# Strassen's seven products for the input projection of layer 0 in a two-layer float32 decoder trunk

## The chip, the core and the metric

The kernel runs on one core of one Trainium2 chip. What is compared is device time in microseconds (us) from launch to end. The core has five engines that run in parallel and wait for each other by semaphores: PE (TensorE, matrix products), DVE (VectorE), ACT (ScalarE), POOL (GpSimd) and SP, whose queue issues the transfers between DRAM and the on-chip memory (SBUF). Products land in PSUM, eight banks of 128 x 512 float32 values, and DVE or ACT read them from there.

## What is computed

The input x has 1024 tokens of 1024 features. Two layers and a last norm follow; only layer 0 changes. Of the reference, cut to what matters:

```python
def even_mixer(y, w_in, w_pool, pool_scale, conv_w, w_out):
    proj = y @ w_in                                   # 1024 x 1024 times 1024 x 6144
    u_a, gate_b, gate_c, h_c, z = jnp.split(proj, [...], axis=-1)
    pooled = causal_multiscale_pool(...)              # four groups, windows 2, 4, 8, 16
    a = jnp.einsum("bsgc,gcd->bsgd", pooled, w_pool).reshape(b, s, POOL_WIDTH) * pool_scale
    cu = gate_c * h_c
    v = conv_w[2] * cu + conv_w[1] * shift_right(cu, 1) + conv_w[0] * shift_right(cu, 2)
    bo = gate_b * v
    out = jnp.concatenate([a, bo], axis=-1) * jax.nn.silu(z)
    return out @ w_out

h = h + even_mixer(rms_norm(h, norm_g[0]), ...)       # layer 0
h = h + odd_mixer(rms_norm(h, norm_g[1]), ...)        # layer 1: sliding-window attention
return rms_norm(h, final_norm_g)
```

Every matrix product is made of float32 values that are split into a high part, rounded to fp32r, and the low rest; ah·bh + ah·bl + al·bh stands for a·b. So one product of a 128 x 128 block of weights with 512 tokens is three matmuls (`mm3`, L178 to L184).

## The kernel before

The projection's 6144 output features are 48 column tiles of 128. A tile of weights is 128 x 8 x 128 (eight blocks of 128 input features); it comes in by one transfer of 512 KB, ACT casts its high part and DVE subtracts for the low part (`split`, L174 to L176). `take` (L285 and on) keeps loads some three tiles and splits one tile ahead of the products.

- Operands of layer 0: x comes in transposed (`xT`, features on the partitions) in 16 loads of 128 x 512 (`load_x`, L354). ACT multiplies by the norm's gain and rounds (`uH`, L359), DVE makes the low part (`uL`, L360). The norm's factor 1/rms of each token is not applied there but later, to the outputs (`r_b`, `r2_b`), since it is one factor a token; the squares for it (L366 to L369) run beside the first products.
- Start: eight matmuls on zeros (`WARM`, L398), then two column tiles on the first 512 tokens, block by block as the loads arrive (L411 to L413), then a third and a fourth tile.
- Then the 48 tiles in an order written out by hand: for each of four pooling groups two tiles of `u` and two gates, for each of eight convolution tiles j the tiles 16+j, 24+j, 40+j, 8+j. `proj` (L386) makes a tile as two halves of 512 tokens, each 8 blocks x 3 matmuls = 24. After a tile DVE multiplies by `r_b` and does the pooling or convolution, ACT the silu, POOL some multiplications. The small products of the pooling groups (`mix`, L482) are 24 matmuls a group. The gated outputs `o` stay in SBUF.
- Output projection: `operands` (L540) splits `o`, then L564 to L566 make 8 tiles x 2 halves, 48 matmuls each.

The order on PE is the program's. DVE, ACT and SP follow the program's order at the start (`order()`, until the loads of x are through); after that a scheduler sets their order when the kernel is built. The rest, layer 1, is not changed.

Of the kernel before, what the change touches and what calls it, by code (L numbers as in the profile page):

```python
# [32 lines left out]
WARM = 8       # matmuls before the first loads arrive, for the clock of the tensor engine  # L33
SQ = 6         # squares of the first half wait for this tile
# [11 lines left out]
# columns of the per-channel parameter array  # L46
# [29 lines left out]
def trunk(ctx, tc, xT, pos, cols, w_in, w_pool, w_out, w_q, w_kv, w_z, b_q, b_kv,  # L76
# [8 lines left out]
    big = ctx.enter_context(tc.tile_pool(name="big", bufs=16))  # L85
    ps = ctx.enter_context(tc.tile_pool(name="ps", bufs=4, space=PSUM))

    # h1 + b_out: per half, 32 features of 512 tokens each
    h1_dram = tc.dram_tile([2, D // 32, HALF, 32], F32, name="h1_dram")

    turn = [0]

    def psA(name=None):
        turn[0] += 1
        return ps.tile([P, HALF], F32, name=name or ("psA", "psD")[turn[0] % 2], bufs=2)

    def psB(dtype=F32):
        return ps.tile([P, HALF], dtype, name="psB")

# [47 lines left out]
    def diag_r(rcol, s):  # L147
        """the 512 values of half s, high and low, on the diagonals of four blocks"""
# [29 lines left out]
    def mm3(dst, parts):  # L178
        """dst = sum over (ah, al, bh, bl) of ah'bh + ah'bl + al'bh."""
# [70 lines left out]
    # ================= layer 0 =================  # L250
    wp = tc.alloc_tile_pool(name="wp", bufs=9, side="right")

    # weights in the order of use: raw tiles are loaded three units ahead, split one unit ahead
    def wtile(shape):
        return lambda d: wp.tile(shape, d, name="W")

    units = []      # (source, raw shape, how to allocate a part, parts)
# [7 lines left out]
    def load_to(n):  # L265
        while len(raws) < min(n, len(units)):
            src, shape, _, _ = units[len(raws)]
            raws.append(wp.tile(shape, F32, name="W"))
# [25 lines left out]
    for m in (32, 33):  # L294
        unit(w_in[m], KP)
    for g in range(1, 4):
        unit(w_in[2 * g], KP)
        unit(w_pool[g - 1], [P, 2, 256])
        for m in (2 * g + 1, 32 + 2 * g, 33 + 2 * g):
            unit(w_in[m], KP)  # L300
    for j in range(8):
        unit(w_in[16 + j], KP)
        if j == 0:
            unit(w_pool[3], [P, 2, 256])
        for m in (24 + j, 40 + j, 8 + j):
            unit(w_in[m], KP)
# [7 lines left out]
    def u_tile(shape):  # L314
        return lambda d: big.tile(shape, d, name="U")
# [4 lines left out]
    for s in range(2):  # L320
        for m in range(KT):
            if s == 0 and m == 0:
                unit(w_z[m], KP, u_tile(KP))
            elif s == 1 and m >= ZLATE:
                unit(w_z[m], KP, lambda d: big.tile([P, 4, P], d, name="O0"), parts=2)
# [8 lines left out]

    order()
    with tc.tile_pool(name="l0", bufs=4) as p0:
        def T():
            return p0.tile([P, 16 + S], F32, name="T", bufs=4)

        def t2(dtype=F32):  # L340
            return p0.tile([P, HALF], dtype, name="t2", bufs=5)

        def big2(s, dtype=F32):
            return big.tile([P, HALF], dtype, name=f"O{s}")

        r_b = p0.tile([P, S], F32, name="r_b", bufs=1)
        r2_b = p0.tile([P, S], F32, name="r2_b", bufs=1)

        uH = [big.tile([P, S], F32R, name="U") for _ in range(KT)]
        uL = [big.tile([P, S], F32R, name="U") for _ in range(KT)]  # L350

        heads, loads = [], []

        def load_x(s, k):  # L354
            xin = big2(s)
            loads.append(nc.sync.dma_start(out=xin, in_=xT[k * P:(k + 1) * P, hs(s)]))
            if s == 0 and k == 0:
                nc.sync.dma_start(out=colt, in_=cols)
            heads.append(act(out=uH[k][:, hs(s)], in_=xin, func=AF.Copy, scale=col(C_G1, k)))  # L359
            stt(out=uL[k][:, hs(s)], in0=xin, scalar=col(C_G1, k),  # L360
                in1=uH[k][:, hs(s)].bitcast(F32), op0=ALU.mult, op1=ALU.subtract)
            return xin

        def squares(xs, add):
            acc = t2()
            act(out=acc, in_=xs[0], func=AF.Square)  # L366
            for x in xs[1:]:
                act(out=x, in_=x, func=AF.Square)
                add(out=acc, in0=acc, in1=x, op=ALU.add)  # L369
            return acc  # L370

        def stats0(s, acc):
            rsqrt_mean(const, rcol0[:, 4 * s:4 * s + 4], col_sums(acc), 4)

        def spread0(s):
            bank = spread_r(diag_r(rcol0, s), psB() if s == 0 else psA())
            nc.scalar.copy(out=r_b[:, hs(s)], in_=bank)
            tt(out=r2_b[:, hs(s)], in0=bank, in1=r_b[:, hs(s)], op=ALU.mult)
# [6 lines left out]
        pre = {}  # L385

        def proj(m):
            if m in pre:
                return pre.pop(m)
            w = take()  # L390
            return [proj_half(w, s) for s in range(2)]

        # keep the tensor engine busy, for its clock, while the first loads arrive
        bank, idle = psB(), t2()[:, 0:HALF // 2]
        nc.vector.memset(idle, 0.0)
        idle = idle.bitcast(BF16)
        for _ in range(WARM):
            mm(bank, lhsT=idle[:, 0:P], rhs=idle, start=True, stop=True)  # L398

        # start: three weight tiles on the first half while the second half arrives  # L400
        ws = [[wp.tile(KP, d, name="W") for d in (F32, F32R, F32R)] for _ in range(2)]
# [603 lines left out]
```

## Time and profile before

| | |
|---|---|
| time, median of 3 runs | 1157.64 us (1156.61 to 1157.99) |
| span of the profiled execution | 1158.2 us, 0.56 us above that median |
| PE busy | 1126.6 us, 97% |
| DVE, ACT, POOL busy | 619.2, 386.6, 272.6 us |
| moved by DMA | 83.92 MB, 72 GB/s over the span |

The page gives the profiled execution's span alone, from the first to the last instruction. Busy time is the union of an engine's instructions; a matmul's shown duration includes its way through the array, so on PE the distance from start to start tells the rate. The granted clock of PE is a share of 2.4 GHz: 1.00 is that level, 0.5 is 1.2 GHz.

### The profile page before, as it was taken

How to read it: one execution, taken by the hardware profiler on the slowest of the kernel's cores; microseconds unless marked ns; L12 is line 12 of the kernel's file. 1: busy time of each engine (PE TensorE's matmuls, PEld its weight loads, DVE VectorE, ACT ScalarE, POOL GpSimd, SP SyncE). 2: the span in 40 equal slices, each digit the busy share in tenths (PEclk: the TensorE clock that was granted, in tenths of full speed). 3: DMA queues.
4: the chain of work that ended last, by engine and by line, in shares of the span. 5: the costliest groups of instructions: out<-in, count | busy, mean ns of one | idle time of the engine just before them, and what ended most of it. 6: DMA issues, size and time to landing. Idle time of an engine off the chain costs nothing.

```text
span 1158.2 us, 14036 instructions
## 1 busy us (share of the span) xinstructions
PE 1126.6 (97%) x5248; PEld 921.5 (80%) x5248; DVE 619.2 (53%) x1109; ACT 386.6 (33%) x797; POOL 272.6 (24%) x427
## 2 busy tenths in 40 slices
PE   9999999999999999999999999999999998898897
PEld 6788888888888888888888788898888886677676
DVE  7993637332233223223655865641133669899995
ACT  8132122111111111111432532420012687776653
POOL 1200000010010110110101100143330036787874
PEclk9899999999999999999999999999999999999999
DMA  7111111111111111111144344520022405460001
GB/s 242 45 47 55 46 52 49 55 41 51 55 37 55 55 37 55 54 38 64 59 148 148 110 164 144 177 80 1 19 69 95 146 19 120 64 90 21 19 19 55
DMA packets 59892, 83.92 MB, mean 72 GB/s; under 512 B 36272, under 2 KB 37424, under 8 KB 59824
## 3 DMA queue, kind: packets, MB, share of 16 engines
q1 hardware_dynamic: 59824, 83.03, 23.4%
q8 instruction: 41, 0.67, 0.2%
q14 instruction: 27, 0.22, 0.1%
HBM read 74.63 MB, written 8.39 MB: 72 GB/s over the span
## 4 chain that ended last, share of the span: by engine, by line
PE 85%; DVE 8%; ACT 3%; issue 1%; DMA 1%; SPq 1%; POOL 0%; ACTq 0%; DVEq 0%
PE psB L184 8%; PE psB L183 8%; PE psB L182 8%; PE psA L184 5%; PE psA L183 5%; PE psA L182 5%; PE psD L184 5%; PE psD L183 5%; PE psD L182 5%; PE psA L566 2%; PE psA L564 2%; PE psA L565 2%; PE psD L566 2%; PE psD L564 2%; PE psD L565 2%
## 5 line engine op out<-in xcount | busy, mean ns | idle before, releaser
L175 ACT CAST W<-W 128x1024 fp32r<-128x1024 f32 (+2 forms) x109 | 107.4, 988 | 531.7 <-DVE W L176 427.0
L176 DVE TENSOR_TENSOR W<-W 128x1024 fp32r<-128x1024 f32 (+2 forms) x109 | 125.4, 1155 | 235.6 <-PE psB L183 177.8
L183 PE MATMUL psB<-U,W 128*128 128x512 f32 x384 | 152.6, 397 | 2.0 <-DVE U L360 1.8
L184 PE MATMUL psB<-U,W 128*128 128x512 f32 x384 | 152.7, 398 | 0.0
L182 PE MATMUL psB<-U,W 128*128 128x512 f32 x384 | 150.7, 392 | 0.0
L183 PEld LDWEIGHTS psB<-U,W 128*128 128x128 f32 x384 | 72.9, 190 | 20.8 <-DVE U L360 4.0
L521 POOL TENSOR_TENSOR T<-T,r_b 128x1024 f32<-128x1024 f32 x8 | 19.3, 2416 | 290.6 <-DVE T L519 290.6
L182 PEld LDWEIGHTS psB<-U,W 128*128 128x128 f32 x384 | 72.9, 190 | 16.4
L184 PEld LDWEIGHTS psB<-U,W 128*128 128x128 f32 x384 | 73.1, 190 | 14.5
L184 PE MATMUL psD<-U,W 128*128 128x512 f32 x184 | 72.5, 394 | 0.0
L184 PE MATMUL psA<-U,W 128*128 128x512 f32 x184 | 72.5, 394 | 0.0
L183 PE MATMUL psD<-U,W 128*128 128x512 f32 x184 | 72.2, 392 | 0.0
L183 PE MATMUL psA<-U,W 128*128 128x512 f32 x184 | 72.1, 392 | 0.0
L182 PE MATMUL psA<-U,W 128*128 128x512 f32 x184 | 71.5, 389 | 0.0
L182 PE MATMUL psD<-U,W 128*128 128x512 f32 x184 | 71.4, 388 | 0.0
L582 POOL TENSOR_TENSOR t<-t,T 128x512 f32<-128x512 f32 x14 | 19.2, 1370 | 170.5 <-ACT T L581 170.5
L734 ACT ACTIVATE pt<-psB,smax 128x128 f32<-128x128 f32 x128 | 45.5, 367 | 25.0 <-DVE smax L731 21.6
L722 PE MATMUL psB<-kT,qT 128*128 128x256 f32 (+1 forms) x128 | 35.2, 297 | 17.3 <-ACT qT L703 9.4
L875 PE MATMUL psD<-O,aH 128*128 128x512 f32 (+1 forms) x128 | 51.1, 399 | 0.0
L566 PE MATMUL psA<-U,W 128*128 128x512 f32 x128 | 50.4, 394 | 0.5 <-DVE W L176 0.5
L566 PE MATMUL psD<-U,W 128*128 128x512 f32 x128 | 50.3, 393 | 0.0
L564 PE MATMUL psD<-U,W 128*128 128x512 f32 x128 | 50.1, 392 | 0.0
(291 smaller groups left out, 2588.0 us busy)
## 6 DMA issues: line engine op xcount, KB each, us to landing
W<-w_in SPq DMA_DIRECT2D x46, 512.0 KB, 3.5
W<-w_out SPq DMA_DIRECT2D x32, 512.0 KB, 3.7
W<-w_z SPq DMA_DIRECT2D x16, 512.0 KB, 3.4
O<-xT SPq DMA_DIRECT2D x16, 256.0 KB, 5.0
T<-xT SPq DMA_DIRECT2D x16, 256.0 KB, 4.2
h_dram<-T SPq DMA_DIRECT2D x16, 256.0 KB, 2.2
W<-w_q SPq DMA_DIRECT2D x8, 512.0 KB, 4.3
U<-h_dram SPq DMA_DIRECT2D x8, 512.0 KB, 5.7
```

The source lines that it names most:

```text
L175: nc.scalar.copy(out=dst_h, in_=src)
L176: sub(out=dst_l, in0=src, in1=dst_h.bitcast(F32), op=ALU.subtract)
L182: mm(dst, lhsT=ah, rhs=bh, start=(i == 0), stop=False)
L183: mm(dst, lhsT=ah, rhs=bl, start=False, stop=False)
L184: mm(dst, lhsT=al, rhs=bh, start=False, stop=(i == n - 1))
L521: ptt(out=v[:, 0:S], in0=v[:, 0:S], in1=r_b, op=ALU.mult)
L564: mm(dst, lhsT=w[k][0], rhs=oHL[f][0], start=(f == 0), stop=False)
L565: mm(dst, lhsT=w[k][0], rhs=oHL[f][1], start=False, stop=False)
L566: mm(dst, lhsT=w[k][1], rhs=oHL[f][0], start=False, stop=(f == 15))
L722: mm(dst, lhsT=lq, rhs=kT[:, 2 * g, lo:(b + 1) * P], start=True, stop=False)
L734: exps.append(act(out=res[g][:, 2 * i2 + i, :], in_=bv[:, i, P:256], func=AF.Exp, scale=0.125, bias=smax[:, at + i:at + i + 1], accum_out= ...
L875: mm(o, lhsT=a[0][:, kk, :], rhs=woH[8 * n + k][:, c], start=(k == 0), stop=False)
```

## The change

Two column tiles make a pair. With the weights of a pair as a 2 x 2 matrix A (tile by half of the input features) and the normed input as a 2 x 2 matrix B (half of the features by half of the tokens), Strassen's scheme (in Winograd's form) needs seven products of the quarter blocks where eight were made: A11·B11, A12·B21, S2·T2, S1·T1, S3·T3, A22·T4, S4·B22. Each is 4 blocks x 3 = 12 matmuls. The S are sums of weights that DVE makes for every pair (four additions of 128 x 512), the T sums of inputs made once; the outputs C11, C12, C21, C22 need five more additions a pair, which DVE makes as it reads PSUM.

- The sums T mix tokens of both halves, so the norm's factor has to be in the operands. x is read token-major (8 loads of 128 x 1024), squared with a running sum on ACT, multiplied by factor and gain on DVE (`normed`), turned by 64 transposes on PE (`turned`) and copied out of PSUM by ACT and DVE. Then ACT and DVE make high and low parts and the T.
- Since B11 and B21 are ready first, the two products of C11 are made ahead for the first six pairs (`AHEAD`, `go_ahead`), two of the pairs before the second half of the tokens is turned. Their sums go to DRAM (`c_dram`) and come back when the pair's turn comes; the weights of those pairs are loaded a second time.
- The gated outputs go to DRAM (`o_dram`, `spill`) and are read back by `operands`.
- The multiplications by `r_b`, those on POOL and the broadcast of the factor fall away.

The heart of the diff:

```diff
-        def proj_half(w, s):
-            dst = psA() if s == 0 else psB()
-            mm3(dst, [(w[k][0], w[k][1], uH[k][:, hs(s)], uL[k][:, hs(s)]) for k in range(KT)])
-            return dst
...
+W_BUFS = 9
+T3_BUFS = 14
+LEAD = 3
+AHEAD = 6
...
+    order_ = ("A11", "S2", "S1", "S3", "A12", "A22", "S4")
...
+            if what == "S2":
+                s1 = pools["t3"].tile([P, 4, P], F32, name="S1", bufs=2) if i else \
+                    T()[:, 0:HALF].rearrange("p (k c) -> p k c", c=P)
+                wsum[i] = s1
+                tt(out=s1, in0=a21, in1=a22, op=ALU.add)
+                tt(out=a21, in0=a11, in1=a21, op=ALU.subtract)
+                tt(out=a11, in0=s1, in1=a11, op=ALU.subtract)
+            if what == "S4":
+                tt(out=a12, in0=a12, in1=a11, op=ALU.subtract)
...
+            hl = W([P, 2, 4, P], F32R)
+            split(hl[:, 0], hl[:, 1], src)
...
+    def product(dst, i, what, b, start=True):
+
+        prepare_to(at[i, what] + 1 + (LEAD if "t3" in pools else 0))
+        w, x = whl[i, what], ops[b]
+        for k in range(4):
+            for n, (hw, hx) in enumerate(((0, 0), (0, 1), (1, 0))):
+                mm(dst, lhsT=w[:, hw, k], rhs=x[hx][:, k], start=start and k + n == 0,
+                   stop=k == 3 and n == 2, skip_group_check=not start)
...
+        b2 = bank()
+        product(b2, i, "S2", "T2")
+        tt(out=u2_, in0=b2, in1=p1, op=ALU.add)
+        b3 = bank()
+        product(b3, i, "S1", "T1")
+        b2 = bank()
+        product(b2, i, "S3", "T3")
+        tt(out=p1, in0=b2, in1=u2_, op=ALU.add)
+        tt(out=o22, in0=b3, in1=p1, op=ALU.add)
+        if i >= AHEAD:
+            product(b1, i, "A12", "B21", False)
+            c11(b1)
+        b4 = bank()
+        product(b4, i, "A22", "T4")
+        tt(out=o21, in0=b4, in1=p1, op=ALU.add)
+        product(b3, i, "S4", "B22", False)
+        tt(out=o12, in0=b3, in1=u2_, op=ALU.add)
...
+    def normed(b):
+        stt(out=xb[b], in0=xb[b], scalar=rcol0[:, b:b + 1], in1=gB, op0=ALU.mult, op1=ALU.mult)
+
+    def turned(b):
+        s, bb = divmod(b, 4)
+        for kh in range(2):
+            bk = bank()
+            for i in range(4):
+                k = 4 * kh + i
+                tr(bk[:, i * P:(i + 1) * P], xb[b][:, k * P:(k + 1) * P], ident)
+            (nc.vector.tensor_copy if kh and b < 4 else nc.scalar.copy)(
+                out=Y[f"{kh + 1}{s + 1}"][:, :, bb * P:(bb + 1) * P],
+                in_=bk.rearrange("p (k c) -> p k c", c=P))
...
+    run(cast("B11", b11))
+    square(4)
+    run(cast("B21", b21))
+    run(low("B11", b11) + low("B21", b21))
+    square(5)
+    go_ahead([lambda: square(6), lambda: square(7),
+              lambda: rsqrt_mean(const, rcol0[:, 4:8], ss[:, 4:8], 4)]
+             + [lambda b=b: normed(b) for b in range(4, 8)], [], [], [])
+    for b in range(4, 8):
+        turned(b)
```

The pairs come in the order U0, CH0, BZ0, CH1, BZ1, Z0, U1, CH2, BZ2, Z1, CH3, BZ3 and so on to CH7, BZ7: U are two pooling tiles of a group, Z its two gates, CH the tiles 16+j and 24+j of a convolution, BZ the tiles 8+j and 40+j. Four `mix` follow the Z.

**ACT at the start.** Before, ACT goes from one block of x to the next and the split of the weights that belong to it (O are loads of `xT`, W weights):

```order
L359 ACTIVATE U<-O_155,colt 128x512
L175 CAST W<-W 128x256 x2
L359 ACTIVATE U<-O_172,colt 128x512
L359 ACTIVATE U<-O_182,colt 128x512
L175 CAST W<-W 128x256 x2
```

Now (T and x are blocks of x, y the turned operands, b a PSUM bank; L506 squares, L518 copies what was turned, L551 copies a C11 sum):

```order
L506 ACTIVATE W,ss_144<-T 128x1024 x4
L179 CAST W<-W 128x512
L518 COPY y_136<-b 128x4x128 x4
L525 CAST B11h<-y_136 128x1024 x2
L506 ACTIVATE W,ss_144<-x_166 128x1024
L525 CAST B21h<-y_137 128x1024 x2
L506 ACTIVATE W,ss_144<-x_170 128x1024
L551 COPY W<-b 128x512
L179 CAST W<-W 128x512 x3
L506 ACTIVATE W,ss_144<-x_172 128x1024
L506 ACTIVATE W,ss_144<-x_174 128x1024
```

One cast of weights stands ahead of the operands' casts; the next three stand behind two squares, two casts of B21 and the copy of the first product's sum.

**DVE at the end of the projection.** Before (L527 multiplies the last tile's two halves out of PSUM; the L176 of U are the low parts of the output projection's operands, first half of the tokens):

```order
L527 TENSOR_TENSOR O_3604<-psD,O_3604 128x512
L176 TENSOR_TENSOR U<-O_593,U 128x512
L176 TENSOR_TENSOR U<-O_599,U 128x512
L176 TENSOR_TENSOR U<-O_849,U 128x512
L176 TENSOR_TENSOR U<-O_911,U 128x512
L176 TENSOR_TENSOR U<-O_1163,U 128x512
L176 TENSOR_TENSOR U<-O_1225,U 128x512
L176 TENSOR_TENSOR U<-O_1479,U 128x512
L176 TENSOR_TENSOR U<-O_1541,U 128x512
L527 TENSOR_TENSOR O_3607<-psB,O_3607 128x512
```

Now (L463, L468, L469, L475, L477 are the five sums of the last pair, in the order of its products; L705, L706 and L711 gate them; the L180 of U are the low parts):

```order
L463 TENSOR_TENSOR t3_4031<-b_4032,t3_4013 128x512
L468 TENSOR_TENSOR t3_4013<-b_4065,t3_4031 128x512
L469 TENSOR_TENSOR t3_4012<-b_4049,t3_4013 128x512
L705 TENSOR_TENSOR t3_4009<-b_4014,T_4005 128x512
L475 TENSOR_TENSOR t3_4011<-b_4097,t3_4013 128x512
L711 TENSOR_TENSOR T_4126<-t3_4011,t3_4009 128x512
L477 TENSOR_TENSOR t3_4010<-b_4049,t3_4031 128x512
L706 TENSOR_TENSOR t3_4010<-t3_4010,T_4005 128x512
L711 TENSOR_TENSOR T_4129<-t3_4012,t3_4010 128x512
L180 TENSOR_TENSOR U_4185<-O0_4152,U_4184 128x512
L180 TENSOR_TENSOR U_4185<-O0_4154,U_4184 128x512
L180 TENSOR_TENSOR U_4191<-O0_4156,U_4190 128x512
```

The eight low parts that stood ahead of the last half's product now all stand behind the last product's sum (L477) and two operations that follow from it.

## Rows read from the trace of the kernel before

**Rows 1.** The page: span, then busy us, share and count of each engine.
```profile
span 1158.2 us, 14036 instructions
PE 1126.6 (97%) x5248; PEld 921.5 (80%) x5248; DVE 619.2 (53%) x1109; ACT 386.6 (33%) x797; POOL 272.6 (24%) x427
```

**Rows 2.** Stretches: busy us and count by engine, granted clock, DMA share, GB/s.
```profile
0.00:5.00 5.00, 3.67 (x9) 1.11 (x9) 1.01 (x3) 2.74 (x5) 1.89 (x26) 1.00 0.57 158
5.00:17.00 12.00, 11.71 (x46) 9.01 (x47) 9.84 (x20) 9.81 (x19) 0.00 (x0) 1.00 0.87 295
...
165.00:265.00 100.00, 100.00 (x439) 82.04 (x438) 45.22 (x55) 16.91 (x21) 5.24 (x6) 1.00 0.16 51
```

**Rows 3.** One line: first products (L411), output projection (L564), times of first and last.
```profile
L411 PE MATMUL psD<-U,W x8: 388/388/796, 4.9 to 16.1; 128*128 128x512 f32 x8
...
L564 PEld LDWEIGHTS psA<-U,W x128: 187/188/189, 566.2 to 732.0; 128*128 128x128 f32 x128
```

**Rows 4.** Timeline of PE, 28 to 41 us: start, duration, [idle before <- whom for].
```profile
28.28 0.50 PE L183 MATMUL psB<-U,W 128*128 128x512 f32 x1 [0.79 <-DVE U L360]
...
30.01 0.69 PE L183 MATMUL psB<-U,W 128*128 128x512 f32 x1 [0.77 <-DVE U L360]
30.51 0.63 PE L184 MATMUL psB<-U,W 128*128 128x512 f32 x1
30.93 0.63 PE L182 MATMUL psB<-U,W 128*128 128x512 f32 x1
...
40.40 0.40 PE L184 MATMUL psB<-U,W 128*128 128x512 f32 x1
```

**Rows 5.** Timeline of PE, 1004 to 1013 us: eight transposes, a wait, and after.
```profile
1004.59 1.06 PE L820 MATMUL psB<-ident,pt 128*128 128x128 f32 x8
1005.41 0.48 PE L875 MATMUL psD<-O,aH 128*128 128x512 f32 x1
...
1008.38 0.39 PE L722 MATMUL psB<-kT,qT 128*128 128x256 f32 x1 [2.02 <-ACT qT L703]
...
1009.66 0.52 PE L875 MATMUL psD<-O,aH 128*128 128x512 f32 x1
...
1012.96 0.39 PE L722 MATMUL psB<-kT,qT 128*128 128x256 f32 x1
```

**Rows 6.** ACT groups up to 600 us: shapes, count, busy us, mean ns.
```profile
L175 ACT CAST W<-W 128x1024 fp32r<-128x1024 f32 x55 | 57.9, 1052 | 345.8 <-DVE W L176 336.9 <-DVE T L468 6.9 <-PE psA L565 1.9
L175 ACT CAST U<-O 128x512 fp32r<-128x512 f32 x16 | 8.4, 617 | 3.3 <-PE psB L183 3.3
```

**Rows 7.** DVE groups up to 600 us, same columns.
```profile
L176 DVE TENSOR_TENSOR W<-W 128x1024 fp32r<-128x1024 f32 x55 | 68.3, 1244 | 184.6 <-PE psB L183 173.9 <-issue 6.2 <-PE psD L565 4.3
L176 DVE TENSOR_TENSOR U<-O,U 128x512 fp32r<-128x512 f32 x16 | 9.8, 690 | 0.3 <-PE psB L183 0.3
L472 DVE SCALAR_TENSOR_TENSOR T<-T 128x1023 f32<-128x1023 f32 x2 | 2.4, 1217 | 0.0
```

**Rows 8.** Timeline of DVE: dense runs at 45, 650 and 669 us.
```profile
45.93 0.19 DVE L219 TENSOR_SCALAR tq<-ah 128x64 f32<-128x64 f32 x1
46.16 0.20 DVE L211 TENSOR_SCALAR tr__1568<-tq 128x64 f32<-128x64 f32 x1
...
650.04 9.08 DVE L176 TENSOR_TENSOR U<-O,U 128x512 fp32r<-128x512 f32 x15
659.04 0.69 DVE L572 TENSOR_TENSOR t<-psD,T 128x512 f32<-128x512 f32 x1
659.64 2.35 DVE L176 TENSOR_TENSOR W<-W 128x1024 fp32r<-128x1024 f32 x2
...
669.64 0.16 DVE L143 TENSOR_TENSOR rs_a<-rs_y 128x4 f32<-128x4 f32 x1
669.84 0.16 DVE L144 SCALAR_TENSOR_TENSOR rs_a<-rs_a,rs_v 128x4 f32<-128x4 f32 x1
```

**Rows 9.** DMA issues: KB each, median us to landing.
```profile
W<-w_in SPq DMA_DIRECT2D x46, 512.0 KB, 3.5
```

More of the change, by code (lines that the diff above doesn't have):

```diff
@@ L324, in trunk @@
             elif s == 1 and m >= ZLATE:
[L325 removed]
+                unit(w_z[m], KP, lambda d: pools["big"].tile([P, 4, P], d, name="O0"), parts=2)
             else:
@@ new lines, in trunk, with bank, add @@
+    ps0 = tc.alloc_tile_pool(name="ps0", bufs=8, space=PSUM)
+    bp = tc.alloc_tile_pool(name="bp", bufs=1)
+    def bank():
+        return ps0.tile([P, HALF], F32, name="b")
+    U, Z, CH, BZ = ({} for _ in range(4))
+    pairs = []
+    def add(d, i, m0, m1):
+        d[i] = len(pairs)
+        pairs.append((m0, m1))
+    for g in range(4):
+        add(U, g, 2 * g, 2 * g + 1)
+        for j in (2 * g, 2 * g + 1):
+            if j % 2 and g:
+                add(Z, g, 32 + 2 * g, 33 + 2 * g)
+            add(CH, j, 16 + j, 24 + j)
+            add(BZ, j, 8 + j, 40 + j)
+        if g == 0:
+            add(Z, g, 32 + 2 * g, 33 + 2 * g)
@@ new lines, in trunk, with warm_up @@
+    for n in ("T2", "B11", "T1", "B22", "B21", "T3"):
+        ops[n] = tuple([bp.tile([P, 4, HALF], F32R, name=f"{n}{'hl'[i]}") for i in range(2)])
+    yp = tc.alloc_tile_pool(name="yp", bufs=1)
+    xp = tc.alloc_tile_pool(name="xp", bufs=1, side="right")
+    Y = {n: yp.tile([P, 4, HALF], F32, name=f"y{n}") for n in ("11", "21", "12", "22")}
+    wu = const.tile([P, 128], F32, name="wu")
+    nc.vector.memset(wu, 0.0)
+    wu = wu.bitcast(BF16)
+    def warm_up(n):
+        wb = bank()
+        for _ in range(n):
+            mm(wb[:, 0:256], lhsT=wu[:, 0:P], rhs=wu, start=True, stop=True)
@@ new lines, in trunk, with cast, low, combine @@
+    HK = (slice(0, 2), slice(2, 4))
+    def cast(n, src):
+        return [lambda k=k: nc.scalar.copy(out=ops[n][0][:, k], in_=src[:, k]) for k in HK]
+    def low(n, src):
+        return [lambda k=k: tt(out=ops[n][1][:, k], in0=src[:, k],
+                               in1=ops[n][0][:, k].bitcast(F32), op=ALU.subtract) for k in HK]
+    def combine(out, a, b, op):
+        return [lambda k=k: tt(out=out[:, k], in0=a[:, k], in1=b[:, k], op=op)
+                for k in HK]
+    def run(steps):
+        while steps:
+            steps.pop(0)()
@@ new lines, in trunk, with go_ahead @@
+    kept, c_bank = {}, {}
+    def go_ahead(*steps):
+        for st in steps:
+            i, what = prods[len(ahead)]
+            j = int(what == "A12")
+            if j == 0:
+                c_bank[i], kept[i] = bank(), W([P, 2, HALF])
+            product(c_bank[i], i, what, ("B11", "B21")[j], j == 0)
+            t = kept[i][:, j]
+            nc.scalar.copy(out=t, in_=c_bank[i])
+            if i:
+                nc.sync.dma_start(out=c_dram[i, j], in_=t)
+                t = c_dram[i, j]
+            ahead[i, j] = t
+            prepare_to(min(len(ahead) + LEAD, 2 * AHEAD + 3))
+            run(st)
@@ new lines, in trunk @@
+    nc.sync.dma_start(out=colt, in_=cols)
+    run(cast("B11", b11))
[7 more added lines that the diff above has]
+    for b in range(4, 8):
+        turned(b)
+    xp.release()
+    tp = tc.alloc_tile_pool(name="tp", bufs=1, side="right", reuse_waits="tile")
@@ new lines, in parts, with half, silu_, z_pair @@
+    def parts(src):
+        res = []
+        for s in range(2):
+            h, lo = t3(F32R), t3(F32R)
+            split(h, lo, half(src, s))
+            res.append((h, lo))
+        return res
+    def half(t, s):
+        return t[:, 16 + s * HALF:16 + (s + 1) * HALF]
+    def silu_(dst, src):
+        act(out=dst, in_=src, func=AF.Silu)
+    def z_pair(i):
+        o = [[t3(), t3()], [t3(), t3()]]
+        pair(i, (o[0][1], o[1][0], o[1][1]), lambda b1: silu_(o[0][0], b1))
+        for d in range(2):
+            for s in range(2):
+                if d or s:
+                    silu_(o[d][s], o[d][s])
+        return o
@@ new lines, in gated @@
+    def gated(g, src):
+        pl = [parts(t) for t in src]
+        mix(g, z_pair(Z[g]), pl)
+    for g in range(4):
+        src = u_pair(g)
+        for j in (2 * g, 2 * g + 1):
+            if j % 2 and g:
+                gated(g, src)
+            v = ch_pair(j)
+            bz_pair(j, v)
+        if g == 0:
+            gated(g, src)
+            with tc.tile_pool(name="rope", bufs=1) as pr, tc.issue_after(spilled[-1].ins):
+                rope_tables(pr)
+                small_loads()
```

420 lines of the change are left out of this document (231 added, 189 removed).

## Prediction

> **What bounds the kernel now.** I read four views, from coarse to fine. The page says PE is busy for 1126.6 of 1158.2 us, DVE for 619.2, ACT for 386.6 [rows 1]. Busy time alone does not say that PE is at its rate, so next come the stretches: in a stretch of 100 us of the projection PE makes 439 matmuls at the full granted clock, one in 0.2278 us, without idle time, while DVE works 45 us and the DMA engines are 16% busy at 51 GB/s [rows 2]. Then the places: the first product starts at 4.9 us, the output projection at 566.2 us [rows 3]. Up to there stand 48 x 48 = 2304 matmuls of the projection and 4 x 24 of the mixes, 2400 x 0.2278 = 546.7 us. So 19.5 of the 566.2 us are not PE's rate: the start, and the stretch from 30 to 40 us where the clock is at half. The stage is bound by the number of matmuls, and what they wait for is only seen near the start.
>
> **Removed.** Seven products of 12 matmuls for each of 24 pairs are 2016 matmuls; the built program has 2016 in `product` and 96 in the mixes, so the change does drop 288, worth 288 x 0.2278 = 65.6 us. All of them lay on the path. The multiplications by the norm's factor go from DVE and POOL; they lay beside PE and are worth nothing there.
>
> **Added at the start, step by step** (times from the span's start, taking before's numbers).
> - Input: no product can start before the first 512 tokens are normed. x0, x1, the gain, x2, x3 are five blocks of 0.524 MB, 2.62 MB, ahead on SP's queue. At 158 GB/s up to 5 us and 295 GB/s after [rows 2] they are in at 5 + (2.62 - 0.79)/0.295 = 11.2 us; the first weights, next in the queue, at 13.0.
> - DVE's next instruction is the low part of those weights: cast 0.62 [rows 6], low part 0.69 [rows 7], so 14.3 us, and only then the 11 dependent steps of the inverse root at 0.20 each [rows 8]: 16.5. Four `normed` (the row next to them is 1.22, [rows 7]; 1.12 from start to start for a width of 1024, half of the 2.35 less one tail, [rows 8]) and two copies of 0.60 between them end at 16.5 + 1.22 + 3 x 1.12 + 1.2 = 22.3. Four transposes of the last block at 0.1025 (eight in 0.82, [rows 5]), a copy of 0.6 and a half cast of B11 of 1.05 [rows 6] put the first product, P0, at 24.4; its last low operand is there at 26.7, and it ends at 27.8.
> - P1's weights are cast on ACT behind two casts of 1.05 for B21, two squares of about 1.25 and the copy of P0: P1 starts at 31.3. PE idles for about 3.5 us before it. P1 to P3 take 3 x 2.734 (12 x 0.2278) and 0.6 for a low part: 40.1.
> - The clock. In this trace waits of 0.79 and 0.77 us within two microseconds stand just ahead of a fall to half rate, with 0.43 us a matmul from 30.0 to 40.4 [rows 4]; a wait of 2.02 us stands ahead of one that lasts from 1009.7 to 1013 [rows 5]. Half rate loses 1 - 0.2278/0.4265 = 0.466 of its time: 4.8 and 1.6 us. A wait of 3.5 us I take to be followed by the longer one, since that too was at the start: 44.9 us. The second half's norm (root, four `normed`, to 41.7) is hidden by it.
> - 32 transposes at 0.1025 add 3.3 us, the eight C11 products of the next four pairs 8 x 2.734 = 21.9. Beside them ACT and DVE make the T operands (some 20 us on DVE). U0's own S2 product starts at 70.1. Bounds: 65.3 if the clock doesn't fall, 75.5 if x comes in at 158 GB/s throughout.
>
> **The steady stage.** 156 products are left, 426.5 us, and the mixes, 21.9: 448.4 us if nothing waits. What it now leans on is DVE. From the eviction of U0's S2 to that of Z1's, DVE has 167 operations of width 512, 16 of 1024, 90 small ones of the rotary tables and nine others; PE has 52 products and a mix, 147.6 us. In dense runs DVE starts an operation of 512 every 0.60 us (15 in 9.0), of 1024 every 1.12, a small one every 0.23 [rows 8]: 100 + 18 + 21 + 1 = 140 us, and some 0.7 us in eight pairs in which the low part of S2 directly follows the sum that its cast needs: 145. So PE still sets the pace by 2%, but not everywhere. In the first six pairs S4 goes into the bank that DVE must have read after S3, with one product, 2.7 us, between; I take 0.5 us a pair, 3 us. In CH2 and BZ2, among the rotary tables, DVE has 47.7 us against PE's 38.3; being three products ahead in the weights covers 8.2 of the 9.4; as that lead is hardly full, 3 us. Together 6 us; bounds 0 (all covered) and 15 (the rival on DVE). Later pairs have 13 to 18 us of DVE against 19.1.
>
> The rule that speaks against this change: the DVE row's mean is 0.690 us for 512 elements [rows 7], but its starts are 0.60 apart [rows 8]. The Trainium skill, "VectorE: DVE Perf Modes" (Terms; Mode 2×_2P; Side-by-side: where the cycles go for N=2048 bf16), has fp32 tensor_tensor at one element a cycle of 0.96 GHz and about 150 cycles of set-up, with each operation drained before the next: 0.70 us for 512, an estimate by that page. By it DVE would have some 158 us in that stretch and be the bound. The trace has the page's duration and not its spacing.
>
> Covered: SP's queue gets 10 sums out and 10 back, 31 gated outputs out and 31 back (256 KB each), six weight tiles again and the gain, 25 MB over some 460 us, 55 GB/s beside 51 at 16% [rows 2]: a third of the DMA engines. A spill waits on SP for DVE, and the next weights behind it; these land in 3.5 us [rows 9] and are first split two to six products (5.5 us or more) after their issue. Were the cover gone, each late tile would cost up to 3.5 us. POOL only sets edges to zero now; nobody waits for it. ACT has nine operations of 0.62 and some silu in 19.1 us.
>
> **The hand-over.** All low parts of the output projection's operands now follow the last pair's L477, L706, L711 on DVE: 0.69 + 2 x 0.70 + 0.69 = 2.8 us after the last product, where before eight were done by then and nothing waited. Behind the eighth stands a low part of weights of 1.12: another 0.6 us. And 1.6 us for the clock after such a wait [rows 5]; 0 and 4.8 are its bounds. In all 5.0.
>
> **The sum.** 70.1 + 448.4 + 6 + 5.0 = 529.5 us where before had 566.2: 36.7 us less. Put the other way: 65.6 gained, 29 given back, 18 of it at the start by waits, transposes and half clock (70.1 less 32.8 of C11 products is 37.3 without product at its rate, against 19.5 in all before), 11 later. What follows is unchanged, apart from 4 MB read back beside a stage at 144 GB/s. The profiled execution goes from 1158.2 to 1121.5; its span lies 0.56 above the median, so the median of 1157.64 goes to 1121.
>
> **Rivals.**
> - *Everything is covered.* The clock stays up, DVE keeps its lead: 65.3 + 448.4 + 0 + 3.4 = 517.1, so 1108.5 us. For it: full clock without idle time over hundreds of us. Against: rows 4 and 5.
> - *DVE is the bound up to Z1.* If spacing equals the rows' durations, 167 x 0.69 + 16 x 1.235 + 22 = 157 us, and 5.6 for the casts, against 147.6: 15 in place of 6, so 1130 us. For it: sums that read their predecessor can't overlap it, and a chain over ACT and back is in every pair. Against: the dense runs of rows 8. From Z1 on PE is bound again either way (232 us of DVE at full durations against 295).
> - *The clock keeps falling, and the kernel gets slower.* Place: the nine pairs U0 to BZ2, where DVE has 95% of PE's time or more. Each wait for a sum or a weight part is followed by 10 us at half, as at 30 us [rows 4], 4.8 us a pair: 43 us, 1164 us. From eight such falls on the gain is gone (36.7/4.8). For it: only 0.79 and 0.77 us of waiting stood ahead of a fall. Against: at half clock a product takes 5.1 us, DVE runs ahead, and the next wait is put off.
>
> That the change doesn't do what it says is excluded by the counts.
>
> **Chances.** The forecast, 1114 to 1127: 0.45. All covered, below 1114: 0.22. DVE bound, or a start or hand-over at the dear end, 1127 to 1145: 0.24. The falling clock or an unforeseen wait that eats all: 0.09, of which 0.06 is slower. 0.2% (2.3 us) is about what a measurement of this kernel can tell from no change. Faster 0.92, the same 0.02, slower 0.06. The range 1106 to 1143 joins the first three cases and the outer bounds (75.5 + 448.4 + 15 + 8.2 = 547.1 gives 1138.5).
>
> **What would show it.** Right: `product`'s 2016 matmuls 0.228 us apart in most of the stage; the first at 24 to 26 us; an idle stretch of some 3 us before the second product and a granted clock of 0.5 behind it; DVE over 85% busy up to about 240 us; the first L801 matmul at 525 to 535 us, some 3 us after the last product. Wrong in a step: first product past 28 us (input), PE idle for more than 10 us between 70 and 240 us (DVE), waits of SP's loads that PE's idle time points to (DMA), or a stage after the hand-over that is longer than before's 592 us. The whole is wrong if PE is not the engine that the stage is made of: then DVE's busy share is near 1 past Z1, or the clock is at half in a tenth of the stage or more.

## The result and the profile after

The changed kernel takes 1136.99 us (median of 4 runs, 1134.87 to 1137.65); the kernel before, run beside it, 1157.49. The ratio is 0.9826 with a 95% interval of 0.9812 to 0.984: 20.5 us less, where I had forecast 36.6 less. The profiled execution has a span of 1135.4 us against a forecast of 1121.5 for it, so 13.9 us have to be found.

The page of the changed kernel, with the shares that answer to [rows 1]:

```profile
span 1135.4 us, 14172 instructions
PE 1078.5 (95%) x5020; PEld 873.1 (77%) x5020; DVE 783.5 (69%) x1392; ACT 463.5 (41%) x961; POOL 224.6 (20%) x396
```

The lines of the products (L440, by their first operand) and of the output projection (L800, L801), with the times of the first and last, answer to [rows 3]:

```profile
L440 PEld LDWEIGHTS b<-B11h,W x192: 186/188/331, 26.1 to 514.6; 128*128 128x128 f32 x192
...
L440 PEld LDWEIGHTS b<-T2h,W x192: 186/188/189, 70.8 to 517.4; 128*128 128x128 f32 x192
...
L800 PE MATMUL psD<-U,W x128: 389/394/628, 531.9 to 706.5; 128*128 128x512 f32 x128
...
L801 PEld LDWEIGHTS psD<-U,W x128: 187/188/329, 534.9 to 706.5; 128*128 128x128 f32 x128
```

The output projection starts at 531.9, 34.5 us earlier than the 566.4 of before's first matmul there, but the end comes only 22.8 us earlier. And up to 531.9 the stage is not what was forecast either: the last product was to end at 524.5. The stretches (columns as in [rows 2]) show why:

```profile
5.00:25.00 20.00, 7.91 (x48) 7.27 (x48) 9.52 (x20) 7.19 (x14) 0.22 (x2) 1.00 0.63 237
...
100.00:240.00 140.00, 139.88 (x600) 112.23 (x599) 123.75 (x262) 48.41 (x83) 0.78 (x7) 1.00 0.26 94
240.00:500.00 260.00, 260.00 (x1118) 209.44 (x1117) 190.17 (x281) 81.39 (x138) 0.67 (x6) 1.00 0.21 75
```

From 240 to 500 us PE is never idle, has the full clock, DVE has slack, and yet PE makes 1118 matmuls in 260 us: 430 in 100 us, where before made 439 [rows 2]. Measured from start to start in the 200 us from 250, one takes 0.2330 us on average, in before 0.2289. (My 0.2278 was 100 us divided by a count that has the matmuls cut off at both edges in it.) No wait stands anywhere in that stretch. So the largest loss is not at the start, not on DVE and not at the hand-over; each matmul takes 4.1 ns longer.

Which operands are slow? The same average, product by product, is 0.2333 us for those with B11, B21, T1, T2 and T3, 0.2346 for B22, but 0.2299 for T4. T4 has the same shape, the same weights' buffers and the same order of matmuls; what differs is that it lies at the other end of SBUF, among the buffers of the right side. The output projection of the changed kernel, whose code and operands' shapes are those of before, is slow as well (0.2333 against 0.2289). That spoke for a theory of place: what counts is where the operands lie in memory. The rivals were contention (DVE, ACT and DMA are busier) and the short products (12 matmuls in a bank instead of 24).

### The profile page after: what moved, and what is told of

It is laid out like the page before. It is cut to its first block, busy times and chain, and to the rows that moved or that the text cites. A ratio compares the mean times of both kernels' runs of the same rounds, so it can differ in the third digit from the quotient of the medians.

```text
span 1135.4 us, 14172 instructions
## 1 busy us (share of the span) xinstructions
PE 1078.5 (95%) x5020; PEld 873.1 (77%) x5020; DVE 783.5 (69%) x1392; ACT 463.5 (41%) x961; POOL 224.6 (20%) x396
## 4 chain that ended last, share of the span: by engine, by line
PE 79%; DVE 12%; ACT 5%; issue 2%; DMA 2%; POOL 0%; SPq 0%; DVEq 0%; ACTq 0%
PE b L440 38%; PE psD L801 3%; PE psD L802 3%; PE psA L800 2%; PE psD L800 2%; PE psA L802 2%; PE psA L801 2%; PE psA L186 2%; PE psD L186 2%; PE psA L187 2%; PE psA L188 2%; PE psD L188 2%; PE psD L187 2%; ACT pt L972 1%; DMA W<-w_in 1%
## 5 line engine op out<-in xcount | busy, mean ns | idle before, releaser
L179 ACT CAST W<-W 128x512 fp32r<-128x512 f32 (+1 forms) x199 | 143.9, 731 | 357.9 <-DVE W L180 108.5
L180 DVE TENSOR_TENSOR W<-W 128x512 fp32r<-128x512 f32 (+1 forms) x199 | 162.6, 823 | 115.2 <-ACT W L179 68.6
L440 PE MATMUL b<-B11h,W 128*128 128x512 f32 x192 | 65.6, 405 | 2.7 <-ACT W L179 1.8
L440 PE MATMUL b<-T2h,W 128*128 128x512 f32 x192 | 64.5, 396 | 2.2 <-ACT W L179 2.2
L440 PE MATMUL b<-B22h,W 128*128 128x512 f32 x192 | 64.7, 398 | 1.2 <-DVE T L469 1.1
L440 PE MATMUL b<-T1h,W 128*128 128x512 f32 x192 | 64.4, 396 | 0.0
L440 PE MATMUL b<-T3h,W 128*128 128x512 f32 x192 | 64.3, 396 | 0.0
L440 PE MATMUL b<-B21h,W 128*128 128x512 f32 x192 | 63.9, 396 | 0.0
L440 PE MATMUL b<-T4h,W 128*128 128x512 f32 x192 | 63.5, 391 | 0.0
L801 PE MATMUL psD<-U,W 128*128 128x512 f32 x128 | 51.5, 402 | 2.6 <-DVE U L180 2.6
L802 PE MATMUL psA<-U,W 128*128 128x512 f32 x128 | 50.4, 394 | 1.4 <-DVE W L180 1.4
L802 PE MATMUL psD<-U,W 128*128 128x512 f32 x128 | 50.9, 398 | 0.2 <-DVE W L180 0.2
L800 PE MATMUL psD<-U,W 128*128 128x512 f32 x128 | 51.1, 399 | 0.0
L800 PE MATMUL psA<-U,W 128*128 128x512 f32 x128 | 50.8, 397 | 0.0
L801 PE MATMUL psA<-U,W 128*128 128x512 f32 x128 | 50.6, 395 | 0.0
```

Source lines behind the costliest of these rows:

```text
L179: nc.scalar.copy(out=dst_h, in_=src)
L180: sub(out=dst_l, in0=src, in1=dst_h.bitcast(F32), op=ALU.subtract)
L440: mm(dst, lhsT=w[:, hw, k], rhs=x[hx][:, k], start=start and k + n == 0, stop=k == 3 and n == 2, skip_group_check=not start)
L800: mm(dst, lhsT=w[k][0], rhs=oHL[f][0], start=(f == 0), stop=False)
L801: mm(dst, lhsT=w[k][0], rhs=oHL[f][1], start=False, stop=False)
L802: mm(dst, lhsT=w[k][1], rhs=oHL[f][0], start=False, stop=(f == 15))
```

## Experiments: the pace of the matmuls

**Thirty-two bytes.** Nothing but the place of the buffers is changed; the order of the instructions stays, with one more that sets an unused tile to zero. In three of the four runs this tile lies ahead of all others on the left side, in one on the right side, where W and T4 are.

```diff
     const = ctx.enter_context(tc.tile_pool(name="const", bufs=1))
+    pad = const.tile([P, 8], F32, name="pad")
+    nc.vector.memset(pad, 0.0)
```

> The changed kernel with 32 unused bytes at the head of the pool const: every buffer on the left side of SBUF (the operands T1, T2, T3, B11, B21, B22 of the products, U of the output projection) starts 32 bytes later, at 96 instead of 64 past a multiple of 128; the weights W and T4 stay at 96. Place theory (the pace of 0.2331 us a matmul instead of 0.2289 comes from where the operands start): 0.229 to 0.230 us a matmul from 300 to 500 us, about 14 us less, 1121 to 1126 us. Contention theory (busier DVE, ACT and DMA slow PE's reads): still 0.233, 1136 to 1138 us. Short-product theory (12 matmuls to a bank instead of 24): the same, 1136 to 1138 us.

The same lines in the kernel before:

> The kernel before with the same 32 bytes: its operands U move from 32 to 64 past a multiple of 128, weights W stay at 96. Place theory: matmuls go from 0.2289 to about 0.233 us, (2304 + 768) x 4.4 ns = 13.5 us and some more in layer 1, 1168 to 1174 us. Contention and short-product theories: no change, 1157 to 1158 us.

On the right side, in the changed kernel:

```diff
+    padr = ctx.enter_context(tc.tile_pool(name="padr", bufs=1, side="right"))
+    nc.gpsimd.memset(padr.tile([P, 8], F32, name="pad"), 0.0)
```

> The changed kernel with 32 unused bytes at the right end of SBUF instead: the weights W move from 96 to 64 past a multiple of 128, T4 too, while the other operands stay at 64. Place theory in the form that the moving operand's start alone counts: still 0.233 us a matmul, and T4's products, now 0.2297, become as slow, 1137 to 1139 us. In the form that weights and operand must start alike within 64 bytes: 0.229 to 0.230 us everywhere, 1121 to 1126 us. Contention theory: 1136 to 1138 us, and T4's products unchanged.

And 64 bytes on the left (`[P, 16]`):

> The changed kernel with 64 unused bytes at the head of const, twice the shift of the first: operands at 0 past a multiple of 128. Place theory with a period of 64 bytes: as without them, 0.233 us a matmul, 1136 to 1138 us. Place theory with a period of 128 bytes: 0.229 to 0.230 us and 1121 to 1126 us possible. Contention theory: 1136 to 1138 us. It also shows whether a longer const pool alone changes anything.

Measured: 1135.61, 1171.92, 1134.76 and 1138.35 us, beside 1155.69 for the kernel before; the second's ratio is 1.0139 (1.0124 to 1.0154). The stretch from 300 to 400 us of the second, the kernel before with 32 bytes more:

```profile
300.00:400.00 100.00, 100.00 (x430) 80.47 (x429) 27.61 (x31) 13.89 (x15) 10.11 (x8) 1.00 0.15 48
```

This line settles two of the three theories. There is no Strassen in this kernel, every bank gets its 24 matmuls, DVE has 28 us of work in 100 and the DMA engines 15%; still PE makes 430 matmuls in 100 us, as slow as the changed kernel. Thirty-two bytes cost 16.2 us. So neither contention nor short products is needed for this pace; place alone brings it about. But the first run says that the place theory in the form "the operands' own start" is too simple: at 96 past a multiple of 128 they are as slow as at 64, 431 in 100 us:

```profile
300.00:400.00 100.00, 100.00 (x431) 80.71 (x430) 75.58 (x111) 32.25 (x54) 0.45 (x4) 1.00 0.22 72
```

The third run fits neither form that I had written: T4's products stayed fast (0.2279), the others did not become so. What it did show was that the first and the third run agree in every operand's average to 0.1 ns, though no buffer lies at the same place in both. What they have in common is the distance between weights and moving operand. Taking the addresses that the built programs give their buffers, and the distance modulo 256 bytes (in the changed kernel T2's high part at 22080 and a W at 192480: 96), I had 64 for before, 96 for the changed kernel and the shifted kernel before, 128 for the first and third run, 160 for the fourth, and 0 for T4 in all. The averages over all such matmuls of a run are 0.2289 us at 64, 0.2335 and 0.2333 at 96, 0.2329 at 128, 0.2342 at 160, and 0.227 to 0.230 for T4.

**Distance 0.** `[P, 40]` in place of `[P, 8]` in the changed kernel:

> The changed kernel with 160 unused bytes at the head of const. What the first four runs share is the distance from a matmul's weights to its moving operand, taken modulo 256 bytes: 64 in the kernel before (0.2289 us), 96 in the changed one and in the shifted kernel before (0.2333), 128 in the runs with 32 bytes at either end (0.2329, alike in both), 160 with 64 bytes (0.234), and 0 for T4's products in all of them (0.228 to 0.230). Here the distance is 96 + 160 = 256, so 0 for all products and the output projection. Distance theory: 0.228 us a matmul from 300 to 500 us, 14 to 16 us less than the changed kernel, 1120 to 1123 us. Theory of the operands' absolute place (their start is 96 past a multiple of 128, as in the run with 32 bytes): 0.233 us, 1134 to 1136 us.

Measured: 1117.77 us, ratio to before 0.9652 (0.963 to 0.9674), so 19 us less than the changed kernel. The same stretch:

```profile
300.00:400.00 100.00, 100.00 (x443) 82.84 (x442) 77.72 (x115) 33.89 (x57) 0.45 (x4) 1.00 0.22 73
```

443 in 100 us, and 0.2268 from start to start over all products of the run, faster than before's. That is somewhat more than the 14 to 16 us expected, since 0.2268 is better than T4's 0.228 that I had gone by. The operands start at 96 past a multiple of 128 here as in the first run, and DVE is as busy; only the distance is another.

**The same for the kernel before.** If 0.2268 us belongs to the distance, the kernel before can have it too (`[P, 48]`, distance 64 + 192 = 256):

> The kernel before with 192 unused bytes at the head of const, so that its distance from weights to operand goes from 64 to 256, that is 0 modulo 256, as in the 160-byte version of the changed kernel. Distance theory: 0.2268 us a matmul instead of 0.2289 (the changed kernel reached that at distance 0), 2.1 ns for 3072 matmuls and some of layer 1, 6 to 9 us less, 1148 to 1151 us. Then Strassen's part of the 39 us between before and the 160-byte version is 30 to 33 us, where my sum had 36.7. If the faster pace of the 160-byte version belonged to Strassen's form: no change, 1156 to 1158 us.

Measured: 1148.89 us, ratio 0.9934 (0.9921 to 0.9948), as the distance theory has it:

```profile
300.00:400.00 100.00, 100.00 (x443) 82.81 (x442) 27.62 (x31) 14.37 (x16) 10.08 (x8) 1.00 0.15 52
```

So at equal distance Strassen's scheme takes the kernel from 1148.89 to 1117.77: 31 us less, or 33 by the two ratios, 0.9934 and 0.9652, each to the kernel before that was run beside it. That is what the change is worth without the accident of its addresses; it lies in the 30 to 33 us expected, and below the 36.7 of my sum.

**The last value.**

> The kernel before with 160 unused bytes at the head of const: distance from weights to operand 64 + 160 = 224, the one multiple of 32 (modulo 256) that no stage of the runs so far has had. Fast so far were 0 and 64; slow were 32, 96, 128, 160 and 192. If distances that lie within 64 of 256 on either side are fast: 0.227 to 0.229 us a matmul, 1149 to 1158 us. If all but 0 and 64 are slow: 0.233 us, 1168 to 1174 us.

Measured: 1171.97 us, ratio 1.0128 (1.0084 to 1.0173), 0.2333 us a matmul:

```profile
300.00:400.00 100.00, 100.00 (x430) 80.51 (x429) 27.58 (x31) 13.89 (x15) 10.08 (x8) 1.00 0.15 48
```

Of the multiples of 32 only 0 and 64 are fast; nearness to 0 is not it. For 32 and 192 there are only some products of layer 1 to go by, in the kernel before 0.2328 us over 292 matmuls and 0.2333 over 192.

## Experiments: the hand-over

The waits at the hand-over of the changed kernel, timeline of PE:

```profile
531.88 0.39 PE L800 MATMUL psD<-U,W 128*128 128x512 f32 x1
534.88 0.79 PE L801 MATMUL psD<-U,W 128*128 128x512 f32 x1 [2.61 <-DVE U L180]
535.47 0.63 PE L802 MATMUL psD<-U,W 128*128 128x512 f32 x1
535.89 0.63 PE L800 MATMUL psD<-U,W 128*128 128x512 f32 x1
...
547.59 0.40 PE L801 MATMUL psA<-U,W 128*128 128x512 f32 x1
549.43 0.51 PE L802 MATMUL psA<-U,W 128*128 128x512 f32 x1 [1.45 <-DVE W L180]
```

and of DVE in the same time:

```profile
532.08 0.69 DVE L477 TENSOR_TENSOR t<-b,t 128x512 f32<-128x512 f32 x1 [0.74 <-PE b L440]
532.80 0.69 DVE L706 TENSOR_TENSOR t<-t,T 128x512 f32<-128x512 f32 x1
533.53 0.69 DVE L711 TENSOR_TENSOR T<-t,t 128x512 f32<-128x512 f32 x1
534.14 4.90 DVE L180 TENSOR_TENSOR U<-O,U 128x512 fp32r<-128x512 f32 x8
...
547.56 0.69 DVE L808 TENSOR_TENSOR t<-psD,T 128x512 f32<-128x512 f32 x1 [2.57 <-PE psD L802]
548.16 1.22 DVE L180 TENSOR_TENSOR W<-W 128x1024 fp32r<-128x1024 f32 x1
```

Three operations of the last pair stand ahead of the first low part, as the order of the instructions had it. The matmuls behind the wait are 0.43 us apart (half clock). And 15 us later the low part of a weights' tile stands behind L808 on DVE, which waits 2.57 us for the first tile's bank, while DVE has nothing to do: PE loses another 1.6 us for it. Two edits on top of the 160-byte version; the first:

```diff
-                    split(h[:, i, :], lo[:, i, :], raw[f + i])
+                    split(h[:, i, :], lo[:, i, :], raw[f + i], ptt if s == f == 0 else tt)
```

> The 160-byte version, with the first two low parts of the output projection's operands on POOL (about 1.5 us each by a row of the kernel before) instead of at the end of DVE's queue. My theory of the hand-over (low parts behind the last pair's L477, L706, L711 on DVE, 2.8 us of wait and a fall of the clock after it): the wait of 2.8 us shrinks to 0.5 to 1.2 us, the stretch at half clock (1.7 us lost) goes with it or stays, so 1.6 to 4 us less. If the wait is really for the loads of the gated outputs from DRAM: no change. The second wait (1.6 us, 15 us later, low part of weights behind L808) stays.

The second, with the first:

```diff
                 if s == 0 and f == 4:
                     split_to(2)
+                if s == 0 and f == 12:
+                    split_to(3)
```

> As the run before, and the third half tile of w_out is split right after the operands, so that its low part stands ahead of the first tile's sum (L808) on DVE. My theory: the second wait of 1.6 us goes too, together 3.2 to 5.6 us less than the 160-byte version, 1115 to 1119 us. If that wait is for the weights' transfer instead: 1.6 to 4 us less, as without this part.

Measured: 1115.84 and 1114.43 us, ratios 0.9638 (0.9606 to 0.967) and 0.9626 (0.9605 to 0.9647), against 0.9652 without. 1.9 and 3.3 us less; the intervals overlap, so the traces have to tell it. PE in the second of the two (the first has the same waits here):

```profile
519.68 0.39 PE L804 MATMUL psD<-U,W 128*128 128x512 f32 x1
520.46 0.50 PE L805 MATMUL psD<-U,W 128*128 128x512 f32 x1 [0.39 <-POOL U L182]
...
521.71 0.50 PE L805 MATMUL psD<-U,W 128*128 128x512 f32 x1 [0.28 <-POOL U L182]
...
523.58 0.50 PE L805 MATMUL psD<-U,W 128*128 128x512 f32 x1 [0.92 <-DVE U L182]
...
528.33 0.50 PE L805 MATMUL psD<-U,W 128*128 128x512 f32 x1 [0.36 <-DVE U L182]
```

The cause of the wait holds: with two low parts on POOL, PE goes on at 520.46, in the middle of what DVE still does for the last pair; so the loads of the gated outputs are not what PE waits for. But my figure for it does not hold. From start to start PE loses 0.55, 0.45, 1.07 and 0.52 us, 2.6 together, where one wait of 2.8 was. What is gained is the half clock, which does not follow these shorter waits (1.7 us). DVE shows a good part of why the wait moved instead of going:

```profile
519.88 0.69 DVE L479 TENSOR_TENSOR t<-b,t 128x512 f32<-128x512 f32 x1 [0.63 <-PE b L442]
520.60 1.60 DVE L708 TENSOR_TENSOR t<-t,T 128x512 f32<-128x512 f32 x1
522.23 0.69 DVE L713 TENSOR_TENSOR T<-t,t 128x512 f32<-128x512 f32 x1
```

and POOL in the same time:

```profile
519.11 2.54 POOL L182 TENSOR_TENSOR U<-O,U 128x512 fp32r<-128x512 f32 x2 [73.03 <-ACT U L181]
```

The multiplication L708, 0.69 us in the changed kernel, takes 1.60 while POOL is at work, so the low parts behind it on DVE come 0.9 us later. The second edit does what was expected: the 1.6 us at the second tile are gone from the trace, 1.4 of them by the medians.

## Experiments: the start

PE at the start of the changed kernel:

```profile
17.09 1.94 PE L517 MATMUL b<-ident,T 128*128 128x128 f32 x8 [14.09 <-DVE T L509]
...
26.08 0.49 PE L440 MATMUL b<-B11h,W 128*128 128x512 f32 x1 [0.88 <-ACT B11h L525]
27.34 0.49 PE L440 MATMUL b<-B11l,W 128*128 128x512 f32 x1 [0.77 <-DVE B11l L528]
...
32.00 0.50 PE L440 MATMUL b<-B11h,W 128*128 128x512 f32 x1 [1.84 <-ACT W L179]
...
70.79 0.50 PE L440 MATMUL b<-T2h,W 128*128 128x512 f32 x1 [2.19 <-ACT W L179]
```

Eight transposes take 1.94 us at 17 us, about twice the time of those in [rows 5], though the row of 5 to 25 us above has a granted clock of 1.00; the second product waits for its weights' cast; the matmuls from 33 to 36 us run at half clock (1.6 us lost). Three edits tried these, the first alone on the 160-byte version, the others on the version with the mended hand-over.

```diff
-    run(cast("B11", b11))
+    run(cast("B11", b11) + low("B11", b11))
+    prepare_to(2)
     square(4)
-    run(cast("B21", b21))
-    run(low("B11", b11) + low("B21", b21))
+    run(cast("B21", b21) + low("B21", b21))
```

> The 160-byte version, and at the start the second product's weights are cast and split straight after B11, ahead of B21. If what stands ahead of the stretch at half clock near 33 us is PE's wait of 1.84 us for these weights: that wait is gone, no half clock before 45 us, 3.0 to 3.7 us less than the 160-byte version alone, PE's first S2 product at about 67 us. If the fall comes from the longer idle time at the start (12 us from 5 to 17): the wait goes but the half clock stays, 1.5 to 2.2 us less. If DVE's later low part of B21 is what decides: no gain, because the third product then waits.

```diff
-WARM = 8
+WARM = 112
```

> The version with the mended hand-over, and 112 instead of 8 matmuls on zeros ahead of the first transposes (PE had nothing to do from 3 to 17 us). If the slow transposes (0.217 us each from 17 to 23 us, 0.107 later) and the half clock near 30 us come from the idle time ahead of them: transposes near 0.11 us, the first product 2 to 3 us earlier, no half clock before 45 us, 2 to 5 us less than the version with the mended hand-over, 1109 to 1112 us. If DVE's norm and the copies alone set the start: 0 to 1.7 us less. If the zeros take longer than I think (they end past 17 us): slower by up to 6 us.

> As the run before, with the earlier cast of the second product's weights as well. At the start alone that cast brought nothing measurable. If what took its gain was the stretch at half clock: now 1 to 2 us less than the run before. If it was DVE's later low part of B21 or another wait: no difference.

Measured: 1117.88 us for the cast alone (ratio 0.9654, 0.9629 to 0.968; without it 0.9652), 1113.38 for the zeros (0.9628, 0.9614 to 0.9642; without them 0.9626), 1110.15 for both (0.9601, 0.9587 to 0.9615).

The cast alone removes the wait ahead of the second product, but the half clock is there as without it, and U0's S2 product starts at 68.0 instead of 68.6 us; the medians show nothing of it. The zeros do for the transposes what was expected:

```profile
1.17 14.37 PE L495 MATMUL b<-wu 128*128 128x256 bf16 x112 [1.17 <-DVE wu L489]
16.46 1.06 PE L519 MATMUL b<-ident,T 128*128 128x128 f32 x8 [0.93 <-DVE T L511]
...
23.77 0.50 PE L442 MATMUL b<-B11h,W 128*128 128x512 f32 x1 [0.88 <-ACT B11h L527]
25.03 0.50 PE L442 MATMUL b<-B11l,W 128*128 128x512 f32 x1 [0.76 <-DVE B11l L530]
25.37 0.76 PE L442 MATMUL b<-B11h,W 128*128 128x512 f32 x2
25.93 0.63 PE L442 MATMUL b<-B11l,W 128*128 128x512 f32 x1
```

Eight in 1.06 us, and the first product 1.6 us earlier than in the version without them. But the clock falls to half at 25.7 us all the same. In the profiled executions U0's S2 starts at 66.2 us, 3.5 us earlier than without the zeros (69.7); the medians show 1.1 us of that and the ratios nothing, so my expectation of 2 to 5 us fails. With both edits there is no half clock before 900 us, S2 starts at 64.2 us, and 3.2 us are gained against the zeros alone, more than the 1 to 2 expected. The times show a gain only for the two together; by S2's start the zeros do something alone as well, but that start also differs by 1.1 us (68.6 and 69.7) between two versions whose instructions up to there are the same. That says where the time goes at the start; it does not say what sets the clock's fall. PE with both edits:

```profile
25.13 0.50 PE L442 MATMUL b<-B11l,W 128*128 128x512 f32 x1 [0.77 <-DVE B11l L530]
25.46 0.62 PE L442 MATMUL b<-B11h,W 128*128 128x512 f32 x2
25.93 0.40 PE L442 MATMUL b<-B11l,W 128*128 128x512 f32 x1
```

In the last two runs the same two waits of 0.88 and some 0.76 us stand at the same place. The fall begins within a microsecond of them with the zeros alone and does not come with both edits; and with the zeros alone the wait for the weights lies behind the fall, not ahead of it. This stays open.

The wait of 2.2 us at 70.79 was not tried. It goes back to SP: DVE's first sum of weights waits for a transfer,

```profile
67.87 0.69 DVE L409 TENSOR_TENSOR T<-W 128x512 f32<-128x512 f32 x1 [1.39 <-DMA W<-w_in]
```

which SP issues at 61.37, directly behind four spills of C11 sums that take from 52.51 to 61.26 because each waits for its sum:

```profile
52.51 8.75 SPq L553 DMA_DIRECT2D c_dram<-W  x4
61.37 0.86 SPq L381 DMA_DIRECT2D W<-w_in  x2
```

The version with all edits, 1110.15 us (ratio 0.9601, 0.9587 to 0.9615), is faster than both kernels: of the 46 us, 7 are to be had in the kernel before by its distance alone (1156.32 to 1148.89), and 39 come with Strassen's scheme and the mended start and hand-over.

## Why the prediction was right in the sign and 16 us off

Its own steps, forecast and measured, in us of the profiled executions:

| step | forecast | measured |
|---|---|---|
| U0's S2 product starts | 70.1 | 70.8 |
| 1968 matmuls from there (156 products, mixes) | 448.4 | 458.5 (at 0.2330) |
| what PE waits in them | 6 | 2.5 |
| hand-over | 5.0 | 6.1 |
| after it, against before | 0 | +5.6 |

The differences are 0.7 + 10.1 - 3.5 + 1.1 + 5.6 = 14.0 us, where 13.9 were to be found; before's first matmul of the output projection is at 566.4, not at the 566.2 of the weights' load that I took, and the rest is rounding.

**The step that failed** is "2400 x 0.2278" and all that rests on it: I carried the duration of a matmul over from before as a property of PE, and "what follows is unchanged" with it. It is a property of the buffers' places as well. And 0.2278 was too low for before itself, where one takes 0.2289 from start to start. Of the 10.1 us that the 1968 matmuls took more than forecast, the step from 0.2289 to 0.2330 shown above accounts for 8.1 and my reading for 2. Behind the hand-over that step accounts, by matmuls matched one to one between the two traces, for 5.1 of the 5.6 us (3.3 in the output projection, 1.2 in the gates, 0.6 in keys and values).

At before's own distance of 64 the changed kernel was not run; 1136.99 less 8.1 and 5.1 makes 1124 us, an estimate. At distance 0 it takes 1117.77. The forecast of 1121 lies 3 us from either. With the addresses that the kernel has, luck has a part: the 1137 us lie in the range of 1106 to 1143, in the part that I had given to "DVE bound, or a start or hand-over at the dear end", but the main cause is none of these.

Among the signs that I had named as wrong, "a stage after the hand-over that is longer than before's 592 us" came: 534.9 to 1135.4 is 600.5. The "waits of SP's loads that PE's idle time points to" came in one place, ahead of U0's S2 product, for 2.4 us.

**The mechanism held**: 288 matmuls less on a path that PE sets. DVE did not become the bound. From 100 to 240 us DVE is 88% busy and PE waits 0.1 us; the 6 us of stalls in the first pairs were 2.5 in all, the longest (1.1 us of idle time) ahead of U0's S4, where I had put one. Eight low parts in 4.90 us are (4.90 - 0.69)/7 = 0.60 from start to start, as in [rows 8]. The Trainium skill, "VectorE: DVE Perf Modes" (Side-by-side: where the cycles go for N=2048 bf16), by which I had estimated 0.70, agrees with this trace in the duration (0.69); as a spacing 0.70 is too long here too. The rival of DVE is out.

**The start was right by errors that cancel.** The first product came 1.7 us late (26.1), since DVE's copies of what was turned wait for transposes that took twice the time that I had priced (1.94 us for eight at 17 us, 1.06 in [rows 5]). The half clock lasted 3.4 us and cost 1.6, not 10.4 and 4.8; "a wait of 3.5 us I take to be followed by the longer one" was wrong, and the wait itself was 2.0. The eight C11 products took 0.8 more, most of it by the pace. And a wait of 2.4 us for U0's weights that I had not seen took back most of what was left. I had written that a spill waits on SP with the weights behind it, and covered it by the products' lead; that lead is not there yet at U0.

**The hand-over** was right in place and cause (2.8 us, three operations of DVE; 1.7 for the clock behind it), and the low part of weights behind it came as 1.6 instead of 0.6 us, in another place: behind L808.

**The rival of the falling clock** did not come: from the first product to the last there is one stretch at half clock.

## What to carry to other kernels

The pace of matmuls that is taken from one kernel need not hold for another whose buffers lie otherwise; here an added tile of 32 bytes in a pool cost 1.4% of a kernel that PE bounds. So before two versions are compared, and before a slower one is explained, count matmuls in a stretch without idle time: if this pace differs, set it alike first and judge the change then. An instruction put on an in-order engine behind one that waits (SP behind a spill, DVE behind a sum from PSUM) is worth looking for at each start and end of a stage, where no lead has been built up.

## What the runs showed of the hardware

Matmuls of 128 x 512 float32r values with a new load of weights for each, at the full clock and without idle time, were 0.2268 us apart where the moving operand's address less that of the weights is 0 modulo 256 bytes in all products of a kernel, 0.2289 at 64, and 0.2329 to 0.2342 at 96, 128, 160 and 224. The distance is not the whole of it: T4's products, at 0 in every run, were slower where the other operands lay at another distance, up to 0.2299 us in the changed kernel. Why the distance matters was not shown. The Trainium skill, "SBUF — State Buffer" (A bandwidth-pool intuition that's wrong (but worth ruling out)), gives PE a second, independent read port for loading weights, by which I would expect no such dependence; these runs show one. "TensorE: Matmul & The Clock Gate" of the Trainium skill (Wait — 56ns, not 53.3ns?) has 215.7 ns for matmuls of 512 columns back to back; here each has a load of weights of 188 ns beside it, and at best they are 226.7 ns apart, in a stretch of 200 us.

In the version with the mended hand-over DVE's L708, with both operands in SBUF, took 1.60 us instead of 0.69 while POOL read SBUF from 519.11 to 521.65, and L479, which reads one operand from PSUM, kept its 0.69 in the same stretch. The Trainium skill, "SBUF — State Buffer" (SBUF: two separate sides), says that DVE operations with two SBUF inputs and GpSimd operations that read SBUF exclude each other; this trace agrees. In the changed kernel, DVE operations of 512 that read the result of the one before started 0.72 and 0.73 us apart (L477, L706, L711), the eight low parts, which do not, 0.60.
